# Expert activations of a PEER stage: gelu, gates and split done in the PSUM bank of the up step, one half of the tokens at a time

## The chip, the cores and the metric

The kernel is one program on one core of a Trainium2 chip. The metric is device time in microseconds (us). The profile names the engines: PE (TensorE, matmuls; PEld its weight loads), DVE (VectorE), ACT (ScalarE), POOL (GpSimd, which also issues the indirect DMAs) and SP (SyncE, which here only issues DMAs). Each engine works through its own list of instructions in order; what one engine needs from another it waits for at a semaphore.

## The reference

One block of a diffusion trunk over 1024 latent tokens of width 1024, in float32: an SSD scan and a Hyena long convolution side by side, an output projection, and then a channel mixing by PEER, a retrieval over 128 x 128 single-neuron experts. The change is in PEER:

```python
q = (hb @ wq).reshape(PEER_BLOCK, PEER_HEADS, 2, PEER_DKEY // 2)
s = jnp.einsum('thsd,snd->thsn', q, subkeys).astype(jnp.float32)
s1, i1 = lax.top_k(s[:, :, 0], PEER_TOPK)
s2, i2 = lax.top_k(s[:, :, 1], PEER_TOPK)
...
gate = jax.nn.softmax(sc, axis=-1).astype(hb.dtype)
u_sel = u_tab[idx]
v_sel = v_tab[idx]
act = jax.nn.gelu(jnp.einsum('td,thkd->thk', hb, u_sel), approximate=False) * gate
return jnp.einsum('thk,thkd->td', act, v_sel)
```

Each token uses 8 heads x 16 = 128 of the 16384 experts.

## The kernel before

The kernel treats the 8 blocks of 128 tokens in two ways. For 3 blocks (`gathered`, L1532) the 128 experts of each token are fetched: an indirect DMA brings one row of 1024 numbers per token (`rows`), and DVE multiplies it with the token (L1544, with the sum) or adds it, scaled, to the result (L1557). There are 3 x 128 rows of the u table and as many of the v table. The running operand `e_p` of both lives in PSUM.

For the other 5 blocks (640 tokens, `TD`) the kernel computes all experts densely, in 128 tiles of 128 experts each, and zeroes the unused ones with a gate matrix G that was spread out before. Per tile, in `score` (L1626) and `up` (L1647):

- `x_raw` (u, transposed) comes in and is split into two fp32r parts `x_uh`, `x_ul` whose sum is the number (L1603, L1604). All dense products are three matmuls of parts.
- For two halves of 320 tokens (`SN` = 2, `SW` = 320): 24 matmuls into `x_s`, a PSUM tile with two buffers (L1643), then a gelu by ACT into one half of the SBUF tile `x_a` (L1644).
- The whole `x_a` (640 columns) is multiplied in place with the gates `x_g` (L1660, DVE), copied to `x_ah` by ACT (L50) and subtracted to give `x_al` by DVE (L51). L50 and L51 are the two lines of `split`.

48 of the 128 tiles (`AHEAD`: the first one or two of each group of four) have their gelu done earlier, beside the routing, and stored in DRAM as `d_A`. For them `up` only loads `x_a` (L1656); the other 80 are scored on the spot. `x_a` has two buffers (`XA`), `x_ah` and `x_al` eight (`AB`).

The down step (`down`, L1674) takes a group of four expert tiles at a time: for each half of the 1024 output columns (A and B below) and each of 5 token blocks, 12 matmuls into an `x_acc` PSUM tile (four buffers), with `x_ah`, `x_al` as weights and the parts `x_vh`, `x_vl` of the v table as moving operand. DVE adds the result to `x_o` (L1689). A v tile is loaded (`x_vr`, two buffers, L1611), copied by ACT (L1614) and subtracted by POOL (L1615) into one of five buffers; a half uses four of them.

`run` (L1719) writes the program of this stage group by group: the 10 units of the down step of group g, with the four ups of group g + 1 before units 2, 5, 7 and 8, and gathered rows spread between them. The framework then schedules: it replays the program on a timeline of its own and fixes each engine's order, so ups, downs and gathers are interleaved on PE and DVE. The stage is the last of the kernel.

Of the kernel before, what the change touches and what calls it, by code (L numbers as in the profile page):

```python
# [10 lines left out]
F32 = mybir.dt.float32  # L11
# [4 lines left out]
AF = mybir.ActivationFunctionType  # L16
# [1121 lines left out]
def mix(K, scan):  # L1138
# [16 lines left out]
    with K.pool("hm") as wk, K.pool("hl") as late, K.pool("hc") as pool, K.pool("hp", space=PSUM) as ps:  # L1155
        H = Hyena(K, pool, ps, wk, late)
        H.matrices(K.nc.gpsimd, "dft_f", "dft_i")
        convs = H.convs()
        with K.pool("sk") as sp, K.pool("skw") as sw, K.pool("skp", space=PSUM) as pk:
            keys = search_keys(K, pk, sp, sw)  # L1160
            with scan:
                beside(both(K.side, keys, KS), CS)
            beside(keys, KR)
        with K.pool("ot") as sp, K.pool("otw") as sw, K.pool("otp", space=PSUM) as ps:
            def raster(t):
                return lambda c: t[c * 128:(c + 1) * 128, :]

            def colmajor(c):
                return colrows(T["h0"], c)

            beside(out_some(K, ps, sp, sw, range(8), T["ossd"], raster(K.i["x"]), raster(T["h0"])), TR)
            if NLW:
                while H.done < NLW:
                    next(convs)
                beside(out_some(K, ps, sp, sw, range(8, 8 + NLW), T["ohy"], colmajor, colmajor), TL)
            for _ in convs:
                pass
# [97 lines left out]
TD = ND * 128  # L1275
NG = NB - ND
NT = 128
GT = 32
# [7 lines left out]
SN = 2 if TD > 512 else 1  # L1286
SW = TD // SN


class Route:  # L1290
# [96 lines left out]
    def second(self, b, wk):  # L1387
# [23 lines left out]
        V.tensor_copy(pof, pos)  # L1411
        up = wk.tile([128, 8, 16], F32, name="r_up", bufs=1)
        V.tensor_scalar(up, pof[:, 0], 4.0, None, op0=ALU.is_ge)
        V.scalar_tensor_tensor(pof[:, 2], pof[:, 2], 12.0, pof[:, 0], op0=ALU.subtract, op1=ALU.subtract)
        V.tensor_sub(pof[:, 3], pof[:, 3], pof[:, 1])
# [67 lines left out]
class Experts:  # L1483
# [24 lines left out]
    def beside(self, x, tiles):  # L1508

        self.some(x)  # L1510
        self.ahead += tiles
        while self.n < min(int(self.ahead), NE):
            self.K.nc.sync.dma_start(self.K.T["A"][self.n], self.score())
            self.n += 1

    def gather(self, table, ids, j):
# [106 lines left out]
        nc.sync.dma_start(t, K.T["G"].rearrange("q p e t -> p q e t")[:, :, e:e + SC, :])  # L1623
        return t

    def score(self):  # L1626

        nc, wk, ps, R = self.K.nc, self.wk, self.ps, self.R
        fh, fl = R.fTd
        if not self.nu:  # L1630
            self.raw_u()
            self.raw_u()
            self.part_u()
        self.raw_u()
        self.part_u()
        uh, ul = self.parts.pop(0)
        a = wk.tile([128, TD], F32, name="x_a", bufs=XA)
        for m in range(SN):
            ms = slice(m * SW, (m + 1) * SW)
            s = ps.tile([128, 512], F32, name="x_s", bufs=2)  # L1640
            for k in range(8):
                for q, (w, x) in enumerate(((uh, fh), (uh, fl), (ul, fh))):
                    nc.tensor.matmul(s[:, :SW], w[:, k], x[:, k, ms], start=(k == 0 and q == 0), stop=(k == 7 and q == 2))  # L1643
            nc.scalar.activation(a[:, ms], s[:, :SW], AF.Gelu)  # L1644
        return a

    def up(self, g, m):  # L1647

        K, nc, wk = self.K, self.K.nc, self.wk
        e = SC * g + m  # L1650
        if m == 0:
            self.g4 = self.gates(e)
            self.A[g] = []
        if e in AHEAD:
            a = wk.tile([128, TD], F32, name="x_a", bufs=XA)
            nc.sync.dma_start(a, K.T["A"][AHEAD.index(e)])  # L1656
        else:
            a = self.score()
        av = a.rearrange("p (q t) -> p q t", t=GT)
        (nc.gpsimd if self.turn('m', MP) else nc.vector).tensor_mul(av, av, self.g4[:, :, m, :])  # L1660
        hi = wk.tile([128, TD], F32R, name="x_ah", bufs=AB)
        lo = wk.tile([128, TD], F32R, name="x_al", bufs=AB)
        K.split(a, hi, lo)
        self.A[g].append((hi, lo))

    def ahead_v(self, n):
# [127 lines left out]
XA = 2  # L1794
UR = 0.5
UP = 0.6
MP = 0
# [136 lines left out]
```

## Time and profile before

| | us |
|---|---|
| three runs | 4242.83, 4247.77, 4251.62 |
| median | 4247.77 |
| the profiled execution | 4236.63 |
| span of its instructions | 4234.9 |
| busy PE / DVE / POOL / ACT | 3766.8 / 3434.8 / 2218.0 / 1373.3 |

The stage described above begins at about 2600 us in the profile, with the first load of a stored `x_a`, and its last down step ends at about 4190 us. A profile's row of a group gives the busy time, the mean of one instruction, and the idle time of its engine just before, with what ended it.

### The profile page before, as it was taken

How to read it: one execution, taken by the hardware profiler on the slowest of the kernel's cores; microseconds unless marked ns; L12 is line 12 of the kernel's file. 1: busy time of each engine (PE TensorE's matmuls, PEld its weight loads, DVE VectorE, ACT ScalarE, POOL GpSimd, SP SyncE). 2: the span in 40 equal slices, each digit the busy share in tenths (PEclk: the TensorE clock that was granted, in tenths of full speed). 3: DMA queues.
4: the chain of work that ended last, by engine and by line, in shares of the span. 5: the costliest groups of instructions: out<-in, count | busy, mean ns of one | idle time of the engine just before them, and what ended most of it. 6: DMA issues, size and time to landing. Idle time of an engine off the chain costs nothing. (4 is left out here: it accounts for less than half of the span.)

```text
span 4234.9 us, 59929 instructions
## 1 busy us (share of the span) xinstructions
PE 3766.8 (89%) x21481; PEld 3307.3 (78%) x21481; DVE 3434.8 (81%) x6389; ACT 1373.3 (32%) x2567; POOL 2218.0 (52%) x1723
## 2 busy tenths in 40 slices
PE   5999999898888887789998877899989999989995
PEld 4787887777877786688998876788878888878884
DVE  5665887556889795599999996798878888878998
ACT  3233333326454121232225665222222222222221
POOL 2232323244344221065737785676767677667675
PEclk9999999998898998899999999999999999999997
DMA  6333433467774546567645546899989999989997
GB/s 209 103 123 103 130 112 133 134 194 223 228 233 142 168 148 180 166 214 250 232 134 206 201 170 218 285 338 322 354 314 340 317 326 340 342 310 341 337 322 258
DMA packets 509674, 974.09 MB, mean 230 GB/s; under 512 B 33771, under 2 KB 291231, under 8 KB 506432
## 3 DMA queue, kind: packets, MB, share of 16 engines
q1 hardware_dynamic: 395616, 557.25, 40.2%
q0 software_dynamic: 110880, 405.98, 26.2%
q10 hardware_dynamic: 2880, 7.03, 0.5%
q8 instruction: 169, 2.77, 0.3%
q14 instruction: 129, 1.06, 0.1%
HBM read 823.20 MB, written 146.95 MB: 229 GB/s over the span
## 5 line engine op out<-in xcount | busy, mean ns | idle before, releaser
L1643 PE MATMUL x_s<-fTh,x_uh 128*128 128x320 f32 x2048 | 640.9, 313 | 12.1 <-ACT x_a L1644 11.9
L1643 PE MATMUL x_s<-fTh,x_ul 128*128 128x320 f32 x2048 | 638.9, 312 | 7.2 <-DVE x_ul L1604 7.2
L1643 PE MATMUL x_s<-fTl,x_uh 128*128 128x320 f32 x2048 | 640.0, 313 | 0.0
L1683 PE MATMUL x_acc<-x_vl,x_ah 128*128 128x512 f32 x1280 | 514.1, 402 | 15.1 <-POOL x_vl L1615 15.1
L1683 PE MATMUL x_acc<-x_vh,x_ah 128*128 128x512 f32 x1280 | 449.8, 404 | 82.7 <-ACT x_vh L1614 60.8
L1520 POOL DMA_INDIRECT rows<-in_peer_u_dram,ids x384 | 415.1, 1081 | 197.3 <-DVE rows L1544 65.1
L1557 DVE SCALAR_TENSOR_TENSOR e_p<-rows,e_a,e_p 128x1024 f32<-128x1024 f32 x381 | 489.8, 1286 | 30.6 <-DMA rows<-in_peer_v_dram,ids 19.2
L1683 PE MATMUL x_acc<-x_vh,x_al 128*128 128x512 f32 x1280 | 509.6, 399 | 0.0
L1544 DVE SCALAR_TENSOR_TENSOR rows<-rows,e_p 128x1024 f32<-128x1024 f32 x384 | 455.5, 1210 | 41.7 <-DMA rows<-in_peer_u_dram,ids 39.6
L1520 POOL DMA_INDIRECT rows<-in_peer_v_dram,ids x384 | 397.7, 1036 | 140.5 <-issue 64.0
L1615 POOL TENSOR_TENSOR x_vl<-x_vr,x_vh 128x512 fp32r<-128x512 f32 x256 | 340.8, 1335 | 190.1 <-ACT x_vh L1614 178.9
L1643 PEld LDWEIGHTS x_s<-fTh,x_uh 128*128 128x128 f32 x2048 | 389.3, 190 | 25.8 <-ACT x_a L1644 16.7
L1643 PEld LDWEIGHTS x_s<-fTh,x_ul 128*128 128x128 f32 x2048 | 389.0, 190 | 17.0 <-DVE x_ul L1604 8.3
L1643 PEld LDWEIGHTS x_s<-fTl,x_uh 128*128 128x128 f32 x2048 | 389.3, 190 | 9.2
L1683 PEld LDWEIGHTS x_acc<-x_vh,x_ah 128*128 128x128 f32 x1280 | 241.9, 193 | 135.5 <-ACT x_vh L1614 67.5
L1683 PEld LDWEIGHTS x_acc<-x_vl,x_ah 128*128 128x128 f32 x1280 | 247.7, 194 | 69.3 <-POOL x_vl L1615 23.5
L1614 ACT ACTIVATE x_vh<-x_vr 128x512 fp32r<-128x512 f32 x256 | 159.7, 627 | 421.8 <-DMA x_vr<-in_peer_v_dram 351.4
L1683 PEld LDWEIGHTS x_acc<-x_vh,x_al 128*128 128x128 f32 x1280 | 247.2, 193 | 48.9
L199 PE MATMUL mm<-xl,whi 128*128 128x512 f32 (+1 forms) x784 | 263.6, 410 | 8.2 <-DVE xl L51 8.2
L199 PE MATMUL mm<-xh,whi 128*128 128x512 f32 (+1 forms) x784 | 263.9, 412 | 7.4 <-DVE acc L235 3.6
L51 POOL TENSOR_TENSOR wlo<-wraw,whi 128x1024 fp32r<-128x1024 f32 (+1 forms) x49 | 121.1, 2473 | 280.9 <-ACT whi L50 260.3
L199 PE MATMUL mm<-xh,wlo 128*128 128x512 f32 (+1 forms) x784 | 263.3, 411 | 0.4 <-POOL wlo L51 0.4
(382 smaller groups left out, 8748.9 us busy)
## 6 DMA issues: line engine op xcount, KB each, us to landing
x_raw<-in_peer_uT_dram SPq DMA_DIRECT2D x128, 512.0 KB
x_vr<-in_peer_v_dram SPq DMA_DIRECT2D x256, 256.0 KB
d_G<-r_st SPq DMA_DIRECT2D x20, 2048.0 KB
x_g<-d_G SPq DMA_DIRECT2D x32, 1280.0 KB
wraw<-in_w_mod_dram SPq DMA_DIRECT2D x32, 1024.0 KB
wraw<-in_w_in_dram SPq DMA_DIRECT2D x24, 1024.0 KB
wk_w<-d_WK SPq DMA_DIRECT2D x24, 1024.0 KB
d_kr<-h_k SPq DMA_DIRECT2D x32, 512.0 KB
```

The costliest lines, as they stand in the source:

```text
L51: (self.nc.gpsimd if pool else self.nc.vector).tensor_sub(lo, src, hi.bitcast(F32))
L199: nc.tensor.matmul(p, w[:, k], x[j][:, k, t0:t0 + n], start=(k == 0 and q == 0), stop=(k == 7 and q == 2))
L1520: nc.gpsimd.indirect_dma_start(out=r, out_offset=None, in_=table, in_offset=bass.IndirectOffsetOnAxis(ap=ids[:, j:j + 1], axis=0))
L1544: nc.vector.scalar_tensor_tensor(r, r, 1.0, f, op0=ALU.mult, op1=ALU.mult, accum_out=d[:, j:j + 1])
L1557: nc.vector.scalar_tensor_tensor(acc, r, a[:, j:j + 1], acc, op0=ALU.mult, op1=ALU.add)
L1614: nc.scalar.activation(hi, raw, AF.Copy)
L1615: self.pace = nc.gpsimd.tensor_sub(lo, raw, hi.bitcast(F32)).ins
L1643: nc.tensor.matmul(s[:, :SW], w[:, k], x[:, k, ms], start=(k == 0 and q == 0), stop=(k == 7 and q == 2))
L1683: self.K.nc.tensor.matmul(p, a[x][:, bs], v[w], start=(m == 0 and q == 0), stop=(m == SC - 1 and q == 2))
```

## The change

- `score` becomes a generator. It takes the place for the gelu as an argument; without one the gelu is written back into `x_s` itself, and `score` hands out one half after the other.
- In `up` there is no `x_a` for scored tiles. Per half of 320 columns: gates times `x_s` into `x_s` (DVE), a copy from `x_s` to half of `x_ah` (ACT), a subtraction of both into half of `x_al` (DVE). The tiles with a stored gelu still load `x_a`; the product with the gates is written to a half of `x_s`, which is taken for that, and the rest is as above. So `x_s` goes round 256 halves in this stage, not 160, and a half of it is free again after the subtraction, not after the gelu.
- `beside` (L1508), which computes the stored tiles, allocates `x_a` itself; its instructions are the same.

```diff
--- before.py
+++ after.py
@@ -1510,7 +1510,10 @@
         self.some(x)
         self.ahead += tiles
         while self.n < min(int(self.ahead), NE):
-            self.K.nc.sync.dma_start(self.K.T["A"][self.n], self.score())
+            a = self.wk.tile([128, TD], F32, name="x_a", bufs=XA)
+            for _ in self.score(a):
+                pass
+            self.K.nc.sync.dma_start(self.K.T["A"][self.n], a)
             self.n += 1
 
     def gather(self, table, ids, j):
@@ -1623,7 +1626,7 @@
         nc.sync.dma_start(t, K.T["G"].rearrange("q p e t -> p q e t")[:, :, e:e + SC, :])
         return t
 
-    def score(self):
+    def score(self, out=None):
 
         nc, wk, ps, R = self.K.nc, self.wk, self.ps, self.R
         fh, fl = R.fTd
@@ -1634,15 +1637,13 @@
         self.raw_u()
         self.part_u()
         uh, ul = self.parts.pop(0)
-        a = wk.tile([128, TD], F32, name="x_a", bufs=XA)
         for m in range(SN):
-            ms = slice(m * SW, (m + 1) * SW)
-            s = ps.tile([128, 512], F32, name="x_s", bufs=2)
+            s = ps.tile([128, 512], F32, name="x_s", bufs=2)[:, :SW]
             for k in range(8):
                 for q, (w, x) in enumerate(((uh, fh), (uh, fl), (ul, fh))):
-                    nc.tensor.matmul(s[:, :SW], w[:, k], x[:, k, ms], start=(k == 0 and q == 0), stop=(k == 7 and q == 2))
-            nc.scalar.activation(a[:, ms], s[:, :SW], AF.Gelu)
-        return a
+                    nc.tensor.matmul(s, w[:, k], x[:, k, m * SW:(m + 1) * SW], start=(k == 0 and q == 0), stop=(k == 7 and q == 2))
+            nc.scalar.activation(s if out is None else out[:, m * SW:(m + 1) * SW], s, AF.Gelu)
+            yield s
 
     def up(self, g, m):
 
@@ -1654,13 +1655,16 @@
         if e in AHEAD:
             a = wk.tile([128, TD], F32, name="x_a", bufs=XA)
             nc.sync.dma_start(a, K.T["A"][AHEAD.index(e)])
+            halves = ((a[:, n * SW:(n + 1) * SW], self.ps.tile([128, 512], F32, name="x_s", bufs=2)[:, :SW]) for n in range(SN))
         else:
-            a = self.score()
-        av = a.rearrange("p (q t) -> p q t", t=GT)
-        (nc.gpsimd if self.turn('m', MP) else nc.vector).tensor_mul(av, av, self.g4[:, :, m, :])
+            halves = ((s, s) for s in self.score())
         hi = wk.tile([128, TD], F32R, name="x_ah", bufs=AB)
         lo = wk.tile([128, TD], F32R, name="x_al", bufs=AB)
-        K.split(a, hi, lo)
+        nq = SW // GT
+        for n, (x, s) in enumerate(halves):
+            nc.vector.tensor_mul(s.rearrange("p (q t) -> p q t", t=GT), x.rearrange("p (q t) -> p q t", t=GT),
+                                 self.g4[:, n * nq:(n + 1) * nq, m, :])
+            K.split(s, hi[:, n * SW:(n + 1) * SW], lo[:, n * SW:(n + 1) * SW])
         self.A[g].append((hi, lo))
 
     def ahead_v(self, n):
```

The schedule is made anew for the whole stage. Three places of it follow. In the names, the number at the end is that of one allocation; the brackets list the engines or DMA queues that an instruction waits for.

DVE before, around tile 62 of the 128, a scored one: product with the gates, one gathered row, split.

```order
L1689 TENSOR_TENSOR x_o_22886<-x_o_22886,x_acc_29002 128x512 [waits PE_49]
L1660 TENSOR_TENSOR x_a_29280<-x_a_29280,x_g_29080 128x640 [waits DVE_49,Activation_49]
L1557 SCALAR_TENSOR_TENSOR e_p_28586<-rows_28796,e_a_28583,e_p_28586 128x1024 [waits DMASW5_49,DVE_49]
L51 TENSOR_TENSOR x_al_29335<-x_a_29280,x_ah_29334 128x640 [waits Activation_49]
L1557 SCALAR_TENSOR_TENSOR e_p_28586<-rows_28813,e_a_28583,e_p_28586 128x1024 [waits DMASW6_49,DVE_49]
L1557 SCALAR_TENSOR_TENSOR e_p_28586<-rows_28816,e_a_28583,e_p_28586 128x1024 [waits DMASW7_49,DVE_49]
```

DVE now, the same tile, both halves:

```order
L1665 TENSOR_TENSOR x_s_29478<-x_s_29478,x_g_29269 128x320 [waits Activation_49]
L1560 SCALAR_TENSOR_TENSOR e_p_28761<-rows_29188,e_a_28758,e_p_28761 128x1024 [waits DMASW0_49,DVE_49]
L51 TENSOR_TENSOR x_al_29471<-x_s_29478,x_ah_29470 128x320 [waits Activation_49]
L1560 SCALAR_TENSOR_TENSOR e_p_28761<-rows_29223,e_a_28758,e_p_28761 128x1024 [waits DMASW1_49,DVE_49]
L1693 TENSOR_TENSOR x_o_22886<-x_o_22886,x_acc_29317 128x512 [waits PE_49]
L1560 SCALAR_TENSOR_TENSOR e_p_28761<-rows_29246,e_a_28758,e_p_28761 128x1024 [waits DMASW2_49,DVE_49]
L1607 TENSOR_TENSOR x_ul_29570<-x_raw_29472,x_uh_29569 128x1024 [waits DMAHW7_49,PE_49,Activation_49]
L1560 SCALAR_TENSOR_TENSOR e_p_28761<-rows_29263,e_a_28758,e_p_28761 128x1024 [waits DMASW3_49,DVE_49]
L1665 TENSOR_TENSOR x_s_29507<-x_s_29507,x_g_29269 128x320 [waits Activation_49]
L1560 SCALAR_TENSOR_TENSOR e_p_28761<-rows_29266,e_a_28758,e_p_28761 128x1024 [waits DMASW4_49,DVE_49]
L51 TENSOR_TENSOR x_al_29471<-x_s_29507,x_ah_29470 128x320 [waits Activation_49]
```

Two instructions became four, each with a wait for ACT, and what ACT does between them (gelu, copy) is done twice.

PE before, where the matmuls of tile 61 begin, the first scored tile of its group after a stored one:

```order
L1643 MATMUL x_s_28942<-fTl_13842,x_uh_28821 128x320
L1643 MATMUL x_s_28942<-fTh_13841,x_ul_28822 128x320
L1643 MATMUL x_s_29165<-fTh_13841,x_uh_28911 128x320 [waits Activation_49]
L1643 MATMUL x_s_29165<-fTl_13842,x_uh_28911 128x320
L1643 MATMUL x_s_29165<-fTh_13841,x_ul_28912 128x320
L1683 MATMUL x_acc_28648<-x_vh_28631,x_ah_28483 128x512 [waits Activation_49]
```

PE now, the same place:

```order
L1687 MATMUL x_acc_29249<-x_vh_29206,x_ah_28951 128x512
L1687 MATMUL x_acc_29283<-x_vl_28977,x_ah_28867 128x512
L1687 MATMUL x_acc_29283<-x_vh_28976,x_al_28868 128x512
L1687 MATMUL x_acc_29283<-x_vh_29206,x_ah_28951 128x512
L1644 MATMUL x_s_29360<-fTh_13841,x_uh_29100 128x320 [waits DVE_49]
L1644 MATMUL x_s_29360<-fTl_13842,x_uh_29100 128x320
```

Before, the tile follows the tile ahead of it directly and waits for a gelu (Activation); now it stands behind a run of `x_acc` matmuls and waits for DVE, whose subtraction frees the half that the stored tile took. Over the stage, the stretches of 48 or more `x_acc` matmuls with no `x_s` between them go from 10 (699 of the 3840 matmuls) to 28 (1811).

SP before, the loads of the stored tiles 48 and 49:

```order
L1656 DMA x_a_27839<-d_A_13822 128x640 [waits DMAHW2_49,DVE_49]
L1611 DMA x_vr_27326<-in_peer_v_dram 128x512 [waits DMAHW7_49,Pool_49]
L1611 DMA x_vr_27352<-in_peer_v_dram 128x512 [waits DMAHW1_49,Pool_49]
L1593 DMA x_raw_28058<-in_peer_uT_dram 128x1024 [waits DMAHW5_49,DVE_49]
L1623 DMA x_g_28226<-d_G_13821 128x20x128 [waits DVE_49]
L1656 DMA x_a_27918<-d_A_13822 128x640 [waits DVE_49]
L1611 DMA x_vr_27438<-in_peer_v_dram 128x512 [waits DMAHW3_49,DMAHW0_49,Pool_49]
```

SP now, the same two:

```order
L1657 DMA x_a_27989<-d_A_13822 128x640 [waits DVE_49]
L1614 DMA x_vr_27062<-in_peer_v_dram 128x512 [waits DMAHW6_49,DMAHW3_49,Pool_49]
L1614 DMA x_vr_27085<-in_peer_v_dram 128x512 [waits DMAHW7_49,DMAHW4_49,Pool_49]
L1614 DMA x_vr_27176<-in_peer_v_dram 128x512 [waits DMAHW6_49,Pool_49]
L1596 DMA x_raw_27606<-in_peer_uT_dram 128x1024 [waits DMAHW1_49,Pool_49]
L1614 DMA x_vr_27182<-in_peer_v_dram 128x512 [waits DMAHW7_49,Pool_49]
L1614 DMA x_vr_27188<-in_peer_v_dram 128x512 [waits DMAHW0_49,Pool_49]
L1614 DMA x_vr_27223<-in_peer_v_dram 128x512 [waits DMAHW2_49,Pool_49]
L1596 DMA x_raw_27724<-in_peer_uT_dram 128x1024 [waits DMAHW5_49,DVE_49]
L1614 DMA x_vr_27453<-in_peer_v_dram 128x512 [waits DMAHW3_49,Pool_49]
L1626 DMA x_g_27987<-d_G_13821 128x20x128 [waits DVE_49]
L1657 DMA x_a_28073<-d_A_13822 128x640 [waits DVE_49]
```

Tile 49 was asked for behind 85 loads of `x_vr` and is now behind 82, tile 48 behind 75 where it was 83. Over the 48 stored tiles the load stands 5.4 loads of `x_vr` earlier on average, and earlier for 41 of them.

## Rows read from the trace of the kernel before

**Rows 1.** The page, chain that ended last, by line

```profile
PE x_acc L1683 9%; DMA x_vr<-in_peer_v_dram 7%; PE x_s L1643 6%; POOL rows L1520 2%; DVE rows L1544 1%; POOL x_vl L1615 1%; DVE e_p L1557 1%; DMA rows<-in_peer_u_dram,ids 1%; DVE x_o L1689 1%; DVE x_a L1660 1%; DMA x_a<-d_A 1%; DMA rows<-in_peer_v_dram,ids 1%; DVE x_al L51 1%; ACT x_vh L1614 0%; DVE x_ul L1604 0%
```

**Rows 2.** 2600 to 4190: busy PE, PEld, DVE, ACT, POOL; clock; DMA share; GB/s

```profile
2600.00:4190.00 1590.00, 1483.99 (x7632) 1297.83 (x7632) 1348.13 (x1566) 393.50 (x636) 1108.48 (x947) 0.97 0.92 326
```

**Rows 3.** Chain that ended last, same stretch, by line

```profile
by line: PE x_acc L1683 24.1%; DMA x_vr<-in_peer_v_dram 17.6%; PE x_s L1643 15.3%; issue 12.2%; POOL rows L1520 5.8%; DVE rows L1544 3.3%; POOL x_vl L1615 3.3%; DVE e_p L1557 3.0%; DMA rows<-in_peer_u_dram,ids 2.5%; DVE x_o L1689 2.3%; DVE 
```

**Rows 4.** Groups by line, same stretch: busy, mean ns, idle before and releasers

```profile
L1683 PE MATMUL x_acc<-x_vh,x_ah 128*128 128x512 f32 x1280 | 449.8, 404 | 82.7 <-ACT x_vh L1614 60.8 <-ACT x_ah L50 12.7 <-DVE x_o L1689 8.6
L1520 POOL DMA_INDIRECT rows<-in_peer_v_dram,ids x384 | 397.7, 1036 | 140.5 <-issue 64.0 <-DVE e_p L1557 57.0 <-DVE rows L1544 5.5
...
L1660 DVE TENSOR_TENSOR x_a<-x_a,x_g 128x640 f32<-128x640 f32 x128 | 162.9, 1278 | 108.8 <-DMA x_a<-d_A 70.2 <-ACT x_a L1644 36.2 <-ACT x_uh L1603 2.5
...
L51 DVE TENSOR_TENSOR x_al<-x_a,x_ah 128x640 fp32r<-128x640 f32 x128 | 144.3, 1135 | 4.8 <-ACT x_ah L50 3.6 <-issue 0.7 <-PE x_acc L1683 0.4
L50 ACT ACTIVATE x_ah<-x_a 128x640 fp32r<-128x640 f32 x128 | 93.5, 737 | 300.0 <-DVE x_a L1660 184.3 <-PE x_acc L1683 77.5 <-issue 15.8
...
L1644 ACT ACTIVATE x_a<-x_s 128x320 f32<-128x320 f32 x160 | 66.4, 430 | 155.1 <-PE x_s L1643 95.1 <-DVE x_al L51 40.4 <-PE x_acc L1683 7.0
```

**Rows 5.** Single tiles, same stretch: min/median/max ns of one instruction

```profile
L1660 DVE TENSOR_TENSOR x_a<-x_a,x_g x128: 809/823/4507, 2609.9 to 4156.9; 128x640 f32<-128x640 f32 x128
...
L51 DVE TENSOR_TENSOR x_al<-x_a,x_ah x128: 808/819/5847, 2612.8 to 4160.0; 128x640 fp32r<-128x640 f32 x128
...
L1689 DVE TENSOR_TENSOR x_o<-x_o,x_acc x310: 670/680/691, 2698.6 to 4189.7; 128x512 f32<-128x512 f32 x155
...
L1557 DVE SCALAR_TENSOR_TENSOR e_p<-rows,e_a,e_p x380: 1273/1290/1291, 2682.7 to 4188.5; 128x1024 f32<-128x1024 f32 x190
...
L1544 DVE SCALAR_TENSOR_TENSOR rows<-rows,e_p x275: 1203/1214/1223, 2616.8 to 3911.3; 128x1024 f32<-128x1024 f32 x138
```

**Rows 6.** Timeline of VectorE: start us, us, instruction

```profile
3300.23 0.81 DVE L1660 TENSOR_TENSOR x_a<-x_a,x_g 128x640 f32<-128x640 f32 x1
3300.97 0.81 DVE L51 TENSOR_TENSOR x_al<-x_a,x_ah 128x640 fp32r<-128x640 f32 x1
...
3309.80 2.67 DVE L1660 TENSOR_TENSOR x_a<-x_a,x_g 128x640 f32<-128x640 f32 x1
...
3336.32 2.31 DVE L1660 TENSOR_TENSOR x_a<-x_a,x_g 128x640 f32<-128x640 f32 x1
...
3339.74 1.73 DVE L51 TENSOR_TENSOR x_al<-x_a,x_ah 128x640 fp32r<-128x640 f32 x1
```

**Rows 7.** Timeline of GpSimd and of ScalarE, same place

```profile
3309.38 2.40 POOL L1604 TENSOR_TENSOR x_ul<-x_raw,x_uh 128x1024 fp32r<-128x1024 f32 x1
...
3334.20 0.75 ACT L1644 ACTIVATE x_a<-x_s 128x320 f32<-128x320 f32 x2
...
3338.72 0.74 ACT L50 ACTIVATE x_ah<-x_a 128x640 fp32r<-128x640 f32 x1 [3.25 <-DVE x_a L1660]
```

**Rows 8.** Timeline of three engines around 3170 us

```profile
3168.86 0.83 DVE L1660 TENSOR_TENSOR x_a<-x_a,x_g 128x640 f32<-128x640 f32 x1 [10.43 <-DMA x_a<-d_A]
3169.54 1.29 ACT L1614 ACTIVATE x_vh<-x_vr 128x512 fp32r<-128x512 f32 x2 [15.95 <-DMA x_vr<-in_peer_v_dram]
...
3170.22 2.08 PE L1683 MATMUL x_acc<-x_vh,x_ah 128*128 128x512 f32 x4 [12.12 <-ACT x_vh L1614]
```

**Rows 9.** Chain in order of time: start us, us, matmuls back to back

```profile
2919.82 7.47 PE x_s L1643 x51
...
3928.44 3.23 PE x_acc L1683 x14
```

**Rows 10.** Waits, same stretch: engine, line, us in total, times, longest

```profile
ACT x_vh L1614 <- DMA x_vr<-in_peer_v_dram: 351.4, 96, 16.0
...
PE x_acc L1683 <- ACT x_vh L1614: 60.8, 18, 12.1
...
PE x_s L1643 <- ACT x_a L1644: 8.1, 5, 3.4
```

## The prediction

> **What bounds the kernel now.** I read the chain of the page first, then the busy times of the stretch that the change touches, then its groups, single tiles, and the timeline. The chain that ended last goes through the dense stage by several engines, none with the bulk: down and up matmuls, the loads of the v table, a little of everything else [rows 1]. From 2600 to 4190 us PE is busy 1484 of 1590 us, the DMA engines 92% and DVE 1348 us, 85%; ACT has 393 and POOL 1108 [rows 2]. So PE can win back at most 1590 - 1484 = 106 us, and two other resources stand close behind it. In the chain of this stretch the matmuls have 39.4%, the x_vr loads 17.6%, the listed DVE lines 3.3 + 3.0 + 2.3% [rows 3]. PE's largest wait is for x_vh, 60.8 us in 18 waits, 3.4 us each [rows 4, 10], and ACT, which makes x_vh, waits 351.4 us for x_vr [rows 10]. Around 3170 us one sees it whole: the x_vr loads are late, ACT idles 15.95 us, PE 12.12 us, and DVE too, 10.43 us, for a stored x_a [rows 8]. DVE is thus a neighbour of the bound: POOL waits 57.0 us for its line L1557 before issuing v rows, and ACT 184.3 us for the product with the gates before it can copy x_ah [rows 4].
>
> **The DVE work.** It loses 128 products of 1278 ns and 128 subtractions of 1135 ns: 162.9 + 144.3 = 307.2 us [rows 4]. Both have a minimum and a median near 815 ns and a maximum of 4.5 and 5.8 us [rows 5]. The long ones stand beside POOL: the product that starts at 3309.80 takes 2.67 us while x_ul runs on POOL from 3309.38 for 2.40 us [rows 6, 7]. The mean excess is 1278 - 823 = 455 ns and 1135 - 819 = 316 ns. Instructions that read one operand from PSUM have none of this: x_o keeps to 670 to 691 ns, L1544 to 1203 to 1223, L1557 to 1273 to 1291 [rows 5].
>
> Their price: (1214 - 680) / 512 = 1.043 ns per column, and 680 - 534 = 146 ns fixed; writing to PSUM, as L1557 does and L1544 doesn't, adds 1290 - 1214 = 76 ns [rows 5]. So a subtraction of 320 columns from PSUM costs 334 + 146 = 480 ns, a product within PSUM 556 ns. The product of a stored tile still reads x_a and x_g from SBUF: 556 ns plus an excess for which no row stands at 320 columns, between none and the whole 455 ns per instruction; I take half, 228 ns, since the instruction is half as long. Sum: 256 x 0.480 + 160 x 0.556 + 96 x 0.784 = 122.9 + 89.0 + 75.3 = 287.2 us, 20 us less. A following instruction starts 0.07 us before the end of the last (0.81 us at 3300.23, the next at 3300.97) [rows 6], which 256 more instructions use for another 18 us: 38 us of DVE's time. With no excess it would be 60 us, with the whole 16 us.
>
> By the Trainium skill (SBUF — State Buffer, "Who interferes with whom") a DVE instruction with two SBUF inputs contends with a GpSimd instruction that reads SBUF, one with at most one does not; the rows agree, and by it the stored tiles keep their excess. Against the change speaks VectorE: DVE Perf Modes, "The TRN2 errata": a fixed 120 cycles for a PSUM source against 58 for an SBUF one. At the page's 0.96 GHz that is an estimate of 65 ns, over 512 instructions 33 us, so that nearly all of the 38 us would go. The rows don't show it: x_a at its fastest has 809 - 640 x 1.043 = 141 ns fixed with both inputs in SBUF, x_o 146 with one in PSUM [rows 5].
>
> What of the 38 us reaches the end? All of it if DVE set the pace, but PE and DMA are fuller. The two lines stand in the chain with about 1% of 4235 us each, some 85 us together [rows 1]; they get 38/307 = 12% cheaper, which is 10 us. That is my value; ends 0 and 38.
>
> **The stored x_a.** DVE waits 70.2 us for these loads [rows 4]. Before, the two x_a buffers go round all 128 tiles; now they serve 48, and SP asks for them 5.4 x_vr loads earlier, about 5.4 x 1590/256 = 34 us. That should take most of the waits away. But at the longest of them the x_vr that PE needed started ACT only 0.7 us later (3169.54 against 3168.86) [rows 8], so PE stops there with or without x_a. I count 8 us; ends 0 and 42, the 1% of 4235 us that these loads have in the chain [rows 1].
>
> **ACT.** 256 copies of 320 columns at about 430 ns (the gelu's row) make 110 us against 93.5: 17 us more [rows 4]. ACT is busy a quarter of the time [rows 2], so nothing by itself. The order matters more: gelu, wait for DVE, copy, twice per tile, and behind a waiting copy stand the x_vh that PE needs. That adds to V's delay, below.
>
> **The longer hold of x_s.** So far a half is free after its gelu, and PE waited 8.1 us in all for that [rows 10]. Now gelu, product, copy and subtraction come first. Tile 62 shows the pace: gelus end at 3334.95, product at 3336.32, copy at 3338.72, subtraction from 3339.74 to 3341.47, 6.5 us in all [rows 6, 7]. Per half, with DVE's lag of 1.37 us before the product: 1.37 + 0.56 + 0.09 + 0.43 + 0.28 + 0.48 = 3.2 us. PE has 24 up matmuls of 7.47/51 = 0.146 us between two uses of a half at the least, 3.5 us, and mostly down matmuls of 3.23/14 = 0.23 us besides [rows 9]; counted out with these two prices the new order leaves over 6 us at all but 9 of 158 places. So little there. After a stored tile it is closer: copy and subtraction wait for PE to finish with an older x_ah, and in seven groups of 30 PE then has only 9 or fewer down matmuls, about 2 us, for 2.7 us of copy, lag and subtraction. I put 4 us on all of this; ends 0 and 40.
>
> **V.** PE's order is coarser: 28 long runs of down matmuls instead of 10. In such a run PE eats a v tile in 15 x 0.23 = 3.4 us, while the stage as a whole has 1590/256 = 6.2 us for one. PE waited 3.4 us per x_vh wait [rows 10], so 18 further runs could cost 18 x 3.4 = 61 us. Against that: counted by v tile, the PE work between the last use of the tile whose buffer it takes and its own first use has a median of 11.3 us before and 11.4 now, with four places under 3 us in both. A run is only split elsewhere; the buffers turn at the same rate. I take 4 us; ends -5 and 61.
>
> **Sum.** -10 - 8 + 4 + 4 = -10 us. The profiled execution took 4236.63 us (span 4234.9); 4227 by the sum. The median of the three runs is 4247.77, 11 us above it; I forecast for the median: 4238.
>
> **Rivals.** (A) *V runs dry, slower.* In the long runs ACT sits at copies that wait for DVE, x_vh comes late, PE stands. Each added x_vh wait costs 3.4 us; four of them eat the gain of 14 that the rest leaves, seven make it slower by more than the measurement's uncertainty (0.2%, 8.5 us), and with ten of the 18 it is 4248 - 14 + 34 = 4268. For it: x_vh is PE's largest wait already. Against: the turn of the buffers is unchanged, and the waits before are spread over short runs too. (B) *PE waits for x_s, slower.* If ACT is held by a late x_vr (351.4 us over 96 waits) while a half is still to be copied, PE loses the work that fills its gaps. At a third of the 158 places 1 us each is 53 us; less the gain, 4287. (C) *No change.* DVE is not what ends PE's waits, and the loads come no sooner for PE, since x_vr is late as well: 4248. (D) *All of the DVE time counts.* -38 - 20 + 4 + 4 = -50: 4198. For it: POOL and ACT wait for DVE some 57 and 184 us, and what frees POOL frees v tiles too.
>
> **How the numbers follow.** Forecast, a gain of 9 to 30 us: 0.30. D: 0.11. C, within 0.2%: 0.24. A: 0.23. B: 0.12. So faster 0.41, same 0.24, slower 0.35. The range reaches from D's 4198 to between A and B, 4278; the likeliest case by itself has 4218 to 4239.
>
> **What would show it.** Right: the two DVE groups fall from 307 to about 287 us, subtractions at 480 ns without long ones, scored products near 556; DVE's wait for stored x_a under 30 us instead of 70; PE's idle time in the stretch 95 us or so; PE's waits for x_s under 20 us, now naming DVE. Wrong: waits of PE for x_vh over 90 us (A), or for DVE's x_al before x_s over 40 us (B), a product within PSUM over 650 ns, or subtractions still with microseconds of excess.

## The result and the profile after

The changed kernel takes 4306.05 us (median of four runs, 4297.72 to 4310.4) against 4249.69 for the kernel before in the same series: a ratio of 1.0135 (95% interval 1.0117 to 1.0152), some 56 us slower. The forecast was 4238, its range 4198 to 4278.

The profiled execution took 4297.72 us, its span 4296.0, which is 61.1 more than before. From the two timelines: the stage begins 4.8 us later (first x_g load at 2604.6 instead of 2599.8), from there to the last down matmul it is 1669.3 us instead of 1588.7, and what follows is shorter, 22.1 instead of 46.4. So 4.8 + 80.6 - 24.3 = 61.1: the loss lies inside the stage. Its row (columns as in [rows 2]):

```profile
2605.00:4274.00 1669.00, 1507.39 (x7680) 1311.68 (x7680) 1292.94 (x1831) 411.39 (x772) 1069.90 (x957) 0.95 0.89 313
```

DVE has become 55 us cheaper (1348.13 to 1292.94) although the stretch is longer. PE is busy 23 us more, with 48 more matmuls in the stretch (7.3 us) and a granted clock of 0.95 instead of 0.97, and its idle time has grown from 1590 - 1484 = 106 to 162 us. The DMA share fell from 0.92 to 0.89. None of these resources became fuller; the engines wait for one another longer. The groups that answer to [rows 4], and the minimum, median and maximum of single tiles, as in [rows 5]:

```profile
L1523 POOL DMA_INDIRECT rows<-in_peer_v_dram,ids x384 | 372.6, 970 | 130.9 <-DVE e_p L1560 49.3 <-issue 49.1 <-DVE x_al L51 6.7
...
L51 DVE TENSOR_TENSOR x_al<-x_s,x_ah 128x320 fp32r<-128x320 f32 x256 | 121.1, 483 | 65.5 <-ACT x_ah L50 65.0
L50 ACT ACTIVATE x_ah<-x_s 128x320 fp32r<-128x320 f32 x256 | 109.2, 436 | 365.5 <-DVE x_s L1665 252.2 <-PE x_acc L1687 112.9
...
L1665 DVE TENSOR_TENSOR x_s<-x_s,x_g 128x320 f32<-128x320 f32 x160 | 79.0, 494 | 143.0 <-ACT x_s L1645 142.7
...
L1665 DVE TENSOR_TENSOR x_s<-x_a,x_g 128x320 f32<-128x320 f32 x96 | 60.4, 639 | 19.5 <-DMA x_a<-d_A 19.2
```

```profile
L51 DVE TENSOR_TENSOR x_al<-x_s,x_ah x256: 473/482/495, 2613.8 to 4233.0; 128x320 fp32r<-128x320 f32 x128
...
L1665 DVE TENSOR_TENSOR x_s<-x_s,x_g x160: 483/493/500, 2624.4 to 4230.8; 128x320 f32<-128x320 f32 x160
L1665 DVE TENSOR_TENSOR x_s<-x_a,x_g x96: 483/492/2111, 2612.8 to 4178.0; 128x320 f32<-128x320 f32 x96
```

The long instructions are gone wherever one operand is in PSUM, and only the stored product, which still reads two SBUF tiles, reaches 2111 ns. PE's waits in that stretch, against [rows 10]:

```profile
PE x_acc L1687 <- ACT x_vh L1617: 104.1, 25, 8.8
PE x_acc L1687 <- POOL x_vl L1618: 25.6, 25, 4.9
PE x_acc L1687 <- ACT x_ah L50: 20.3, 2, 17.3
PE x_acc L1687 <- DVE x_o L1693: 15.1, 12, 4.0
PE x_s L1644 <- DVE x_al L51: 4.3, 2, 3.9
```

Not x_s, for which a buffer might be missing, but x_vh: 60.8 to 104.1 us. One place shows how (start, us, instruction; four timelines of the changed kernel). First SP:

```profile
3528.54 0.33 SPq L1596 DMA_DIRECT2D x_raw<-in_peer_uT_dram  x1
3528.96 0.39 SPq L1626 DMA_DIRECT2D x_g<-d_G  x1
3529.70 7.05 SPq L1614 DMA_DIRECT2D x_vr<-in_peer_v_dram  x1
...
3537.68 20.08 SPq L1614 DMA_DIRECT2D x_vr<-in_peer_v_dram  x4
```

Then ACT, DVE and PE:

```profile
3530.65 0.63 ACT L1617 ACTIVATE x_vh<-x_vr 128x512 fp32r<-128x512 f32 x1 [1.26 <-DMA x_vr<-in_peer_v_dram]
3545.60 0.63 ACT L1617 ACTIVATE x_vh<-x_vr 128x512 fp32r<-128x512 f32 x1 [14.31 <-DMA x_vr<-in_peer_v_dram]
...
3552.51 0.77 ACT L50 ACTIVATE x_ah<-x_s 128x320 fp32r<-128x320 f32 x2 [4.82 <-PE x_acc L1687]
```

```profile
3526.88 0.49 DVE L1665 TENSOR_TENSOR x_s<-x_a,x_g 128x320 f32<-128x320 f32 x1
...
3532.21 0.48 DVE L1665 TENSOR_TENSOR x_s<-x_a,x_g 128x320 f32<-128x320 f32 x1
...
3549.25 0.69 DVE L1693 TENSOR_TENSOR x_o<-x_o,x_acc 128x512 f32<-128x512 f32 x1 [8.73 <-PE x_acc L1687]
...
3554.03 0.88 DVE L51 TENSOR_TENSOR x_al<-x_s,x_ah 128x320 fp32r<-128x320 f32 x2
```

```profile
3546.28 2.07 PE L1687 MATMUL x_acc<-x_vh,x_ah 128*128 128x512 f32 x4 [7.70 <-ACT x_vh L1617]
...
3548.58 0.63 PE L1687 MATMUL x_acc<-x_vh,x_al 128*128 128x512 f32 x1
...
3553.01 0.39 PE L1687 MATMUL x_acc<-x_vh,x_al 128*128 128x512 f32 x1
```

At the turn of a group SP issues x_raw (512 KB), x_g (1280 KB) and then the x_vr that PE needs next. That issue alone stands 7.05 us, the data is there 15.9 us after the issue began, and PE idles 7.70 us. In the meantime PE could have scored a tile. It can't: a stored tile put its two products into the two x_s banks at 3526.88 and 3532.21, its copies wait for an x_ah that PE frees only after the late x_vh (3552.51), and the subtractions end at 3554.5 and 3554.9. One bank was held for 28 us, the other for 23, with no matmul in them. The stop also costs clock: PE was busy until 3538.6, then idle, and from 3546.3 to 3552 the granted clock is 0.50, the lower level of 1.2 GHz, with the matmuls 0.43 us apart. From 3552.3 to 3560 it is 1.00 and they are 0.23 us apart.

This is no single place: each of the 22 issues on SP that stand over 4 us in the stage comes directly after an x_g, and so do all 24 in the kernel before. Matched one by one through the two timelines and the order of the instructions, a stored half holds its bank 8.2 us on average from product to subtraction (38 of 96 over 8 us), a scored half 2.65 us (4 of 160 over 8 us).

The start of the stage shows the same once, in the open. PE before:

```profile
2591.52 0.39 PE L1643 MATMUL x_s<-fTh,x_uh 128*128 128x320 f32 x1
...
2611.54 0.80 PE L1683 MATMUL x_acc<-x_vh,x_ah 128*128 128x512 f32 x1 [12.74 <-ACT x_ah L50]
```

and after:

```profile
2613.86 0.80 PE L1687 MATMUL x_acc<-x_vh,x_ah 128*128 128x512 f32 x1 [17.34 <-ACT x_ah L50]
```

Before, the 48 matmuls of the first scored tile (7.3 us) run while the first down step waits. Now both banks belong to stored tiles and the wait is empty.

### The profile page after: what moved, and what is told of

It is laid out like the page before. It is cut to its first block, busy times and chain, and to the rows that moved or that the text cites. A ratio compares the mean times of both kernels' runs of the same rounds, so it can differ in the third digit from the quotient of the medians.

```text
span 4296.0 us, 60124 instructions
## 1 busy us (share of the span) xinstructions
PE 3788.9 (88%) x21481; PEld 3318.7 (77%) x21481; DVE 3359.6 (78%) x6645; ACT 1386.3 (32%) x2695; POOL 2157.6 (50%) x1723
## 5 line engine op out<-in xcount | busy, mean ns | idle before, releaser
L1687 PE MATMUL x_acc<-x_vh,x_ah 128*128 128x512 f32 x1280 | 452.5, 409 | 139.9 <-ACT x_vh L1617 104.1
L1523 POOL DMA_INDIRECT rows<-in_peer_u_dram,ids x384 | 392.9, 1023 | 194.4 <-DVE rows L1547 61.7
L1523 POOL DMA_INDIRECT rows<-in_peer_v_dram,ids x384 | 372.6, 970 | 130.9 <-DVE e_p L1560 49.3
```

What stands on the lines that cost most here:

```text
L1523: nc.gpsimd.indirect_dma_start(out=r, out_offset=None, in_=table, in_offset=bass.IndirectOffsetOnAxis(ap=ids[:, j:j + 1], axis=0))
L1687: self.K.nc.tensor.matmul(p, a[x][:, bs], v[w], start=(m == 0 and q == 0), stop=(m == SC - 1 and q == 2))
```

## The experiments

Three suspects: **H** (**O**, **B** in later runs), the stored tiles hold both x_s banks and coarsen PE's order; **P** (**S** later), the work in halves makes ACT and DVE wait for each other in front of x_vh; **X**, the x_g transfer holds up x_vr. A fourth, **L**, that x_a loads crowd out x_vr, fell with the first run. All ratios are to the kernel before, run beside each.

**One part at a time (E1, E2, E3, E5).** E1: scored tiles as changed, stored ones as before:

```diff
+        if e in AHEAD:
+            a = wk.tile([128, TD], F32, name="x_a", bufs=XA)
...
+            nc.vector.tensor_mul(av, av, self.g4[:, :, m, :])
+            K.split(a, hi, lo)
+        else:
+            for n, s in enumerate(self.score()):
...
```

> Only the scored tiles keep the changed form (gelu, product, copy, subtraction in the bank, half by half); the 48 stored tiles work whole in SBUF as before and take no x_s bank. Theory H (hold): the stored tiles, which take both x_s banks until their subtraction, rob PE of up matmuls to put between down matmuls, so that a late x_vh stops it. In this kernel's PE order there are 9 runs of 48 or more down matmuls (before 10, after 28), so H expects the loss gone: 4215 to 4252 us, PE's wait for x_vh 50 to 70 us. Theory P (ping-pong): the alternation of ACT and DVE over halves delays x_vh in ACT's list; 160 of 256 halves still do it, so some 62% of the +56 us stay: about 4285 us. Theory L (x_a loads asked for earlier crowd out x_vr): the x_a ring still serves stored tiles alone, so 4285 to 4306.

Measured: 4248.31, ratio 1.0002 (0.9988 to 1.0016). The loss is gone, as H said; PE's wait for x_vh is 72.4 us, just over H's 50 to 70. P and L miss by some 36 us or more. DVE's saving (1294.63 us busy in the stage) doesn't show in the total either. In the profiled execution the stage is still 27 us longer than before (1616 against 1589, from the first x_g load to the last down matmul), and what follows it 17.5 us shorter. One wait is new: the new schedule brings the gates late, which neither the kernel before nor the changed one shows.

```profile
DVE x_a L1662 <- DMA x_g<-d_G: 43.9, 9, 8.8
```

E2 is the other half: stored tiles through the banks, scored ones whole in `x_a`.

> The other half of the change alone: the 48 stored tiles take two x_s banks and go half by half, the 80 scored tiles work whole in x_a as before. The PE order has 27 runs of 48 or more down matmuls. H: the loss is there, 4285 to 4315 us, PE's wait for x_vh 85 to 110 us. P: 96 of 256 halves, 38% of +56: about 4271. L: the x_a ring goes round all 128 tiles as before: about 4250.

Measured: 4391.5, 1.0339 (1.0318 to 1.0361), far beyond every theory. Two shortages meet here, which were not tried apart: `x_a`'s two buffers serve all tiles and the banks are held too. DVE waits 122.1 us for stored tiles and PE 38.0 us for a bank:

```profile
DVE x_s L1663 <- DMA x_a<-d_A: 122.1, 16, 19.9
```

```profile
PE x_s L1644 <- DVE x_al L51: 38.0, 7, 11.9
```

E3 keeps the halves and drops the banks (`halves = range(SN)` or `self.score(a)`, product and split on slices of `a`).

> Half by half as in the change, for all tiles, but gelu, product, copy and subtraction read and write x_a in SBUF; x_s is free after the gelu as before. The PE order has 8 runs of 48 or more. H: no loss, 4240 to 4260 us. P: the whole loss, 4290 to 4310. The DVE groups, with two SBUF operands again, should show their long instructions again: sum of product and subtraction 290 to 330 us, against 260 in the changed kernel.

Measured: 4299.16, 1.0126 (1.0102 to 1.015). It is P's number, and H misses. But P is not the only reason for it: with two SBUF operands the half instructions take 814 and 789 ns instead of 494 and 483, 398 us in all, where I had said 290 to 330; DVE is busy 1428 us. How much of the loss each of the two makes E3 can't tell.

```profile
L1667 DVE TENSOR_TENSOR x_a<-x_a,x_g 128x320 f32<-128x320 f32 x256 | 203.0, 814 | 149.2 <-DMA x_a<-d_A 96.8 <-ACT x_a L1645 52.1 <-ACT x_vh L1617 0.3
...
L51 DVE TENSOR_TENSOR x_al<-x_a,x_ah 128x320 fp32r<-128x320 f32 x256 | 195.4, 789 | 13.7 <-ACT x_ah L50 12.9 <-issue 0.4
```

E5 is the changed kernel with one expression altered, so that a stored tile works in halves but in SBUF:

```diff
-  self.ps.tile([128, 512], F32, name="x_s", bufs=2)[:, :SW]) for n in range(SN))
+  a[:, n * SW:(n + 1) * SW]) for n in range(SN))
```

> Scored tiles half by half in the bank as in the changed kernel; stored tiles half by half too, but in x_a in SBUF, so that they take no x_s bank. The PE order has 8 runs of 48 or more down matmuls, as the kernel that leaves stored tiles whole (9, 4248 us). Theory H (stored tiles hold the banks): 4240 to 4265 us, PE idle time 100 to 125 us. Theory S (it is the split of a stored tile into halves, two copies on ACT that each wait for DVE in front of x_vh): 4285 to 4310, PE idle 140 to 160 us, as the kernel with all halves in SBUF (4299).

Measured: 4278.34, 1.0059 (1.0044 to 1.0075): between H and S. Against the changed kernel the bank costs 28 us; against E1 the halves cost 30. These 30 are not those of the changed kernel: the stored halves, with both operands in SBUF, take DVE 123 us here, 23 more than E1's whole tiles, where the changed kernel takes 107. And as in E1 the gates come late:

```profile
DVE x_a L1665 <- DMA x_g<-d_G: 50.6, 12, 9.0
```

**The gates' transfer (E4, E6, E7, E8).** E4 loads the gates per expert tile (`[:, :, e:e + 1, :]`, eight buffers).

> The changed kernel, with the gates of a group loaded in four transfers of 320 KB (one per expert tile, eight buffers of a quarter) instead of one of 1280 KB. The PE order is as coarse as in the changed kernel, 29 runs of 48 or more. Theory X (burst): the loss is the product of the coarse order and of the x_vr issues that stand 4 to 16 us behind an x_g transfer; with shorter transfers no issue on SP takes over 4 us, PE's idle time in the stretch falls from 142 to 60 to 90 us, and the time to 4230 to 4255. H or P without the burst: 4295 to 4310, idle time unchanged.

Measured: 4341.6, 1.0229 (1.0206 to 1.0251), worse. The quarter by experts cuts each piece from 512 to 128 bytes. The row of the changed kernel, then that of E4:

```profile
DMA packets 509675, 974.10 MB, mean 227 GB/s; under 512 B 33771, under 2 KB 291231, under 8 KB 506432
```

```profile
DMA packets 756972, 974.12 MB, mean 224 GB/s; under 512 B 362987, under 2 KB 538527, under 8 KB 753728
```

The same bytes keep the DMA engines busy 0.95 x 1715 = 1629 us of the stage instead of 0.89 x 1669 = 1485. With that price in it the run answers nothing on X. E6 to E8 quarter by tokens instead and issue a quarter in each `up` of the group ahead:

```diff
+            if g + 1 < NT // SC:
+                self.gn = self.gates(e + SC)
...
+            self.gates_part(self.gn, SC * (g + 1), m * nq, nq)
```

> The changed kernel; the gates of a group come in four transfers of 320 KB in pieces of 512 bytes as before, one beside each of the four ups of the group ahead, into the same two buffers. 26 runs of 48 or more. Theory X (the x_g transfer of 1280 KB holds up the x_vr issue behind it, and the coarse order turns that into idle time): no issue on SP over 5 us, PE idle 150 -> 70 to 100 us, 4225 to 4260 us. If the burst is not the cause: 4295 to 4315.

> The kernel before with the same four transfers. X: the gain is smaller, since less of PE's idle time (92 of 104 us against 133 of 150) is there to win: 4205 to 4240 us, and the changed kernel with four transfers stands at most 25 us above it. If the burst is not the cause: 4245 to 4260, and the distance of some 55 us stays.

> Scored tiles in the bank half by half, stored tiles whole in SBUF as before, and the four transfers. H and X together: without the holding of banks and without the burst the DVE time saved has a chance to count: 4190 to 4235 us. If the stage is bound by the sum of PE and DMA work all the same: 4235 to 4255.

Measured, in this order: 4318.15 (1.0152, 1.0134 to 1.0171), 4257.38 (1.0015, 1.0005 to 1.0025), 4248.28 (0.9999, 0.9985 to 1.0012). X seems refuted, but the edit did not do what it was for. SP in E6, four issues in one row:

```profile
3297.30 9.53 SPq L1628 DMA_DIRECT2D x_g<-d_G  x4
3306.93 7.01 SPq L1614 DMA_DIRECT2D x_vr<-in_peer_v_dram  x1
```

The four parts wait for one buffer and go out together: in all 31 groups of E6 their issues begin within 9.4 us, and some 20 x_vr loads still reach ACT over 15 us after their buffer is free. X stayed open.

**The transfer taken away (E9, E10, E17, E18) or put elsewhere (E11, E12).** In the first four the load of the gates has an `if g == 0:` ahead of it.

> The changed kernel, but the gates x_g are loaded for the first group of tiles alone and used for all groups: 31 loads of 1280 KB are left out. Theory X (an x_vr load queued right behind x_raw and x_g on SP lands 15 to 22 us after its buffer is free, and the coarse order of the changed kernel has PE waiting there): loads over 15 us disappear, PE's wait for x_vh falls from 104 to under 50 us, and the time is within 20 us of the same edit on the kernel before. Theory O (the order itself: with the x_s banks held, PE has no up matmuls at the boundary of a group and waits for x_vh with or without a burst): it stays 40 us or more above it.

> The same edit on the kernel before. 40 MB less of some 518 MB in the stage at 326 GB/s is 123 us of transfer; if transfers bound the stage, 4130 to 4180 us; if PE's work does (1484 us of the 1590), PE's idle time of 104 us can at most halve: 4190 to 4210.

> Gates loaded for the first group alone and used for all (31 loads left out); scored tiles in the bank half by half, stored tiles whole in SBUF. One run of 48 or more, as the kernel before with that edit (4130 us; the changed kernel with it has 19 and takes 4168). B (the 38 us come from stored tiles holding the banks): 4115 to 4140. S (from the work in halves on DVE and ACT): 80 of 128 tiles still do it, 4148 to 4160.

> The same with the stored tiles half by half in SBUF, so that all 128 tiles go in halves and none of the stored ones takes a bank; one run of 48 or more. B: 4120 to 4145. S: 4160 to 4175.

E11 and E12 only change the issuing engine:

```diff
-        nc.sync.dma_start(t, K.T["G"].rearrange(...)[:, :, e:e + SC, :])
+        nc.scalar.dma_start(t, K.T["G"].rearrange(...)[:, :, e:e + SC, :])
```

> The changed kernel with the x_g load issued by ACT, on a DMA queue of its own; everything else on SP as it was, the PE order as coarse as in the changed kernel (28 runs of 48 or more). X: x_vr no longer stands behind 1280 KB in one queue, loads over 15 us fall from 19 to under 6, PE's wait for x_vh from 104 to under 60 us, 4240 to 4275 us. O: unchanged order, 4290 to 4315. Against both: ACT has to wait for x_g's buffer before it issues, and x_vh stands behind it.

> The kernel before with the x_g load issued by ACT. X: less to win than in the changed kernel, 4215 to 4245 us. O: 4245 to 4255.

E13 and E14 put E1 and E5 on that queue:

> x_g on ACT's DMA queue; scored tiles in the bank half by half, stored tiles whole in SBUF as before. 9 runs of 48 or more (the changed kernel on that queue 28, 4221 us; the kernel before on it 10, 4184 us). Theory B (the 37 us that are left between those two come from the stored tiles holding both x_s banks): 4175 to 4195 us. Theory S (they come from the work in halves on DVE and ACT): 80 of 128 tiles still do it, 4200 to 4215.

> The same, with the stored tiles half by half in SBUF; no bank taken, 10 runs of 48 or more. B: 4175 to 4200. S: as the changed kernel on that queue, 4212 to 4230.

All medians, in us:

| tiles | x_g on SP | no x_g loads | x_g on ACT |
|---|---|---|---|
| before | 4249 | 4130 (E10) | 4184 (E12) |
| scored in the bank, stored whole in SBUF | 4248 (E1) | 4106 (E17) | 4293 (E13) |
| the same, stored in halves in SBUF | 4278 (E5) | 4117 (E18) | 4317 (E14) |
| the change: stored in the bank too | 4306 | 4168 (E9) | 4221 (E11) |

Ratios with intervals: E9 0.9806 (0.978 to 0.9832), E10 0.9727 (0.9702 to 0.9752), E17 0.9667 (0.9648 to 0.9687), E18 0.9688 (0.9669 to 0.9706), E11 0.9937 (0.9915 to 0.9959), E12 0.9853 (0.9828 to 0.9877), E13 1.011 (1.0093 to 1.0128), E14 1.016 (1.0144 to 1.0176).

Without the loads the changed kernel stands 38 us above the one before, close to O's 40 and past X's 20 (the five runs of E9 spread over 17 us). PE's wait for x_vh falls to 14.6 us and the late loads disappear, as X said. The kernel before gains 119 us by the same edit, close to the 123 that its expectation gave for the transfers. The middle column is the clean one: in the others the gates come late in some variants and not in others. There scored tiles in the bank gain 4130 - 4106 = 24 us; halves for the stored ones cost 10, little more than the scatter; their banks cost 4168 - 4117 = 51. E17 and E18 lie 9 and 3 us below B's ranges. So without the loads S falls and B stands: E18 does all 256 halves and is still faster than the kernel before (E10). PE's waits in E9, then in E18:

```profile
PE x_acc L1688 <- ACT x_ah L50: 21.0, 2, 17.6
PE x_s L1644 <- DVE x_al L51: 15.0, 10, 3.2
PE x_acc L1688 <- ACT x_vh L1617: 14.6, 11, 2.3
```

```profile
PE x_acc L1688 <- ACT x_ah L50: 10.5, 1, 10.5
PE x_s L1644 <- DVE x_al L51: 8.8, 6, 2.9
...
PE x_acc L1688 <- ACT x_vh L1617: 2.3, 2, 1.5
```

Every one of these waits is shorter where the banks are free. X stands as well, with a smaller share: the queue alone, with the same bytes, is worth 65 us to the kernel before and 85 to the changed one, both more than X had said, so some 20 of the 56 us between them go with it and 37 stay. PE's wait for x_vh in E11 and in E12, against 104.1 and 60.8:

```profile
PE x_acc L1687 <- ACT x_vh L1617: 25.9, 13, 5.4
```

```profile
PE x_acc L1683 <- ACT x_vh L1614: 14.0, 11, 3.7
```

The x_vr loads that ACT waits for and gets over 15 us after their buffer is free were 11 before, 13 in E1, 17 in E5, 19 in the changed kernel; in E9, E11 and E12 there is one each at most. The Trainium skill (DMA: Bandwidth & Descriptors, "Queues, rings and completion order") says that a DMA engine takes packets in turn from the rows that have work, and that SP and ACT own a row each; E11 and E12 agree.

E13 and E14 miss every range, B's and S's alike, and can't decide between them: they are far slower than E11, the changed kernel on that queue. They answer something else. DVE of E13:

```profile
DVE x_a L1662 <- DMA x_g<-d_G: 159.9, 22, 12.5
```

ACT issues x_g in its turn, here too late, and the first tile of a group stands for it (E14: 158.7 us in 25 waits); in E11 DVE waits 30.9 us for x_g in all. A queue of its own is bought with a place in the list of an engine that waits.

**A third bank (E15, E16).** Both are E11 with `PA = 3`; E15 has `bufs=3` for `x_s` in this stage, E16 two.

> The changed kernel on ACT's queue for x_g, with a third x_s bank in the dense stage, for which x_acc gives up one of its four (so three each). 14 runs of 48 or more. B: a scored tile always finds a bank beside a stored one, so the waits go: 20 to 40 us below the control with three x_acc banks and two x_s banks. S: no difference to the control beyond 10 us.

> Control: the changed kernel on ACT's queue for x_g with three x_acc banks and still two x_s banks; 27 runs of 48 or more. One bank less for x_acc leaves PE fewer open sums, so 4220 to 4250 us in either theory; only the distance to the kernel with the third x_s bank counts.

Measured: 4234.95, 0.9965 (0.9953 to 0.9977), and 4278.47, 1.0069 (1.0055 to 1.0084). The third bank is worth 44 us, just over B's 20 to 40, and the runs of 48 or more down matmuls fall from 27 to 14. The control lies higher than I expected: the x_acc bank was needed too.

Of the versions that load all gates E11, E12 and E15 beat both kernels. The fastest is E12, the kernel before with x_g on ACT's queue: 4184.3 us, 1.5% below the kernel before.

## Why the prediction was wrong

**The DVE work: right in size, and of little use.** 256 subtractions at 483 ns (said 480), scored products at 494 (556), stored at 639 (784): 260.5 us instead of 287.2. That DVE's time counts in part may be right in kind: E17 takes 24 us less than E10. But DVE's wait for a stored x_a also falls there, from 41.7 to 6.2 us, and the two weren't separated. In the profiled executions 12.6 of 18.9 us lie behind the last down matmul, where DVE in E10 still had the last block of gathered rows to finish, and 6.7 in the stage. In E1, with late gates and late x_vr, the total shows nothing.

**The stored x_a: right in the row, wrong in the end.** DVE's wait for it fell from 70.2 to 19.2 us, as said (under 30). The 8 us can't be seen in the total: DVE now waits 142.7 us for gelus and 65.0 for copies, where it was 36.2 and 3.6 [rows 4].

**ACT: right.** 109.2 us for 110. And x_vh was not late for standing behind waiting copies, as rival A pictured it: at none of PE's 23 stops over 0.5 us for x_vh had ACT just finished something else; it was idle and waiting for x_vr.

**The longer hold of x_s: the step that failed.** "I put 4 us on all of this; ends 0 and 40." It is 28 us in the changed kernel (against E5, which has the late gates besides, so rather more), 51 without the gate loads (E9 less E18), 44 by the third bank (E16 less E15). All of the loss is in the stored tiles: between E1, where they are as before, and the changed kernel lie 58 us, of which this hold is one part and their work in halves the other. Of the 3.2 us per half 1.8 lay behind the lag of 1.37; scored halves took 2.65 from product to subtraction, stored ones 8.2: their copy waits for an x_ah, and x_ah is freed by PE, which stands at the same turn of the group. The step looked for PE's wait at x_s, and this is 4.3 us, under the 20 it named. Rival B had the loss itself, "PE loses the work that fills its gaps", with a chance of 0.12, but looked for it at the same place, as over 40 us of such waits. The price is paid elsewhere: with both banks held, a scored tile's 48 matmuls, which could fill a wait of PE, come after it, as at the two places shown.

**V: its size follows from that.** "I take 4 us; ends -5 and 61"; PE's wait for x_vh rose by 43.3 us, past the 90 us named as the sign for rival A. The text saw the 28 long runs and dismissed them, since the v buffers turn at the same rate. That holds for PE's side of the turn. The load's side was taken as constant, though [rows 8] showed one that took ACT 15.95 us of waiting. What the sum didn't have at all is the reason for these: x_g, with x_raw before it, ahead of x_vr in one queue. Nor did it have the clock that a stop costs PE.

**What stays open.** With the gate loads on SP the halves of stored tiles cost 30 us (E5 less E1), without them 10. DVE has over 20 us more work for them in both cases, and with the gate loads x_vr is late at 17 places instead of 13. What makes it later wasn't separated, and what the halves cost in the changed kernel itself, where the subtraction reads PSUM, stays open. Nor was x_raw moved: it stays on SP in every run, so that its part, if it has one, is in the 37 us that are left and not in the 20.

## What to carry to other kernels

A PSUM bank that is taken as a workplace by something that never was a matmul's result takes work from PE, and the trace may then show hardly any wait for the bank (4.3 us here), only longer waits for whatever that work used to cover; look at what PE runs in its gaps before lengthening a buffer's life. Price a small load by what stands ahead of it in its queue, not by its median. And if one part of a change gains and another loses, as here 24 and 51 us, try the parts alone.

## What the runs showed of the hardware

- A product within PSUM costs DVE 494 ns for 320 columns and a subtraction from PSUM into SBUF 483: 11 ns between them, not the 76 that [rows 5] gave for a write to PSUM at 1024 columns. In E3, with all operands in SBUF, the medians are 484 and 483: no price for a PSUM source. Only the means, 814 and 789, are longer there.
- The same transfers as 128-byte pieces instead of 512 kept the DMA engines busy some 144 us longer in the stage (E4).
- An issue of 256 KB on SP directly behind a 1280 KB transfer stood up to 15.7 us; on a queue without it, in E11, none over 1.4 us.
- The matmuls of 512 columns that followed PE's stop of 7.70 us ran at a granted clock of 0.50, 0.43 us apart; those from 3552.3 us on, at 1.00, 0.23 us apart.
